# Convolution outputs and z gates of a hybrid decoder layer: ScalarE's Silu function in place of tanh and products

## The chip, the cores and the metric

The kernel runs on one core of a Trainium2 chip, in one launch. The metric is the device time of that launch in microseconds (us). TensorE is called PE below, VectorE DVE, ScalarE ACT, GpSimd POOL and SyncE SP, as in the profile.

## The reference, cut to what matters

One layer of a hybrid decoder for 512 prompt tokens and 8 sequences of 8 sample tokens, 576 columns in all, with a width of 1024. One projection of the normed input feeds two groups of heads: a Mamba-2 group (SSD: z, x, B, C, dt) and an RWKV-7 group. What the change touches is the activation behind the causal convolution and the gate z:

```
z, xbc, dt_raw, rw = jnp.split(proj, IN_SPLITS, axis=-1)
conv = depthwise_conv4(concat(conv_buf, xbc)) + conv_b
xbc_act = jax.nn.silu(conv)                       # x, B, C of the SSD group
...
yg = y.reshape(b, l, SSD_WIDTH) * jax.nn.silu(z)  # gate, then a grouped norm
```

Around it stand the chunked SSD scan, the RWKV-7 recurrence in chunks (a triangular solve among them), W_out, a SwiGLU block, a gated per-layer embedding and a last norm. All of it is in fp32; each fp32 operand of a large product is split into a high and a low part, and three matmuls are summed.

## The kernel before, in words

A tile has 128 channels on the partitions and the 576 tokens along the free axis. `projections()` (line 65) lists the 128-channel tiles of the input projection in the order in which PE makes them. The RWKV group is done in four quarters of heads, called q0 to q3 here; each has tiles of its own, and between them stand tiles of the SSD group: 12 convolution tiles `("xbc", c)`, one dt tile, and 8 z tiles. `FILL = (5, 5, 3, 0)` gives q0 four convolutions and dt, q1 five, q2 three. The z tiles come last: some within q3, some at the start of the SSD part.

A quarter runs `prep` (line 529: the lora tiles of decay, a and gate, with Tanh and Exp on ACT, and the scan of the log decay on DVE, line 561, whose result `lo` ACT turns into `pb` with Exp), `gram` (line 601), `bonus`, `decayed`, `inverse` (line 921, with the triangular solve on DVE in `solve`, lines 674 and 676), `chain` (line 739, the recurrence over chunks) and `head_norm`. In `prep` and `gram` the filler tiles give PE dense work between small operations of DVE, ACT and POOL; in q0 and q1 the last fillers lie beside DVE's solve. The chain of one quarter overlaps the preparation of the next. So there are three stretches, one for each of q0, q1 and q2, in which PE waits often.

The kernel is written with the Tile framework, whose scheduler simulates a timeline and sets the order of every engine's queue from it; only the order in which the code is written and the buffers of the pools steer it. A change in the code can therefore move instructions that it does not name. Each engine works through its own queue in order: an instruction that waits holds up all behind it.

A convolution tile (`conved`, line 376) takes the projection out of PSUM into `E` (two ACT copies, 128x512 and 128x64), POOL puts the old state in front and copies the new state `cso` out, ACT makes the first tap `h`, DVE adds three taps (line 395). The SiLU of v is written as (tanh(v/2) + 1) * v/2: the weights and the bias in `hw` are halved at the start (line 172), so `h` is v/2; ACT makes `th` = Tanh(h); DVE forms (th + 1) * h in two pieces, 512 prompt columns (line 400) and 64 sample columns (line 401), into E's place, and a DMA writes it out. E, h and th share a pool of three buffers (`cslot`, line 278), so a convolution holds all three until that DMA is done.

A z tile (`zed`, line 404) goes the same way without a convolution: an ACT copy with scale 0.5 (`hz`), an ACT Tanh with scale 0.5 (`thz`), a DVE product (line 411), and a DMA. ACT's functions need a table; `ACT_TABLE_LOAD` in the queue switches it. Tanh and Exp are used here without a load between them, Ln and the square roots have loads of their own. All calls of ACT go through the helper on line 93, so its instructions all carry L93.

Of the kernel before, what the change touches and what calls it, by code (L numbers as in the profile page):

```python
# [10 lines left out]
AF = mybir.ActivationFunctionType  # L11
ALU = mybir.AluOpType
# [4 lines left out]
P = 128  # L17
D = 1024
NT = 576
ND = 64  # L20
# [55 lines left out]
def hybrid_step(ctx, tc, A):  # L76
    nc = tc.nc
    V, S, G, T = nc.vector, nc.scalar, nc.gpsimd, nc.tensor
# [9 lines left out]
    def nm(s):  # L88
        uid[0] += 1
        return f"{s}_{uid[0]}"  # L90

    def act(out, in_, func=AF.Copy, scale=1.0, bias=0.0):
        return S.activation(out, in_, func, bias=bias, scale=scale)  # L93
# [9 lines left out]
    def lin_bank():  # L103
        turn[0] += 1
        return lins[turn[0] // 2 % len(lins)].tile([P, 1024], F32, tag="lin", name=nm("lin"))

    def lin_ps(off=224):
        return lin_bank()[:, off:off + NT]
# [8 lines left out]
    def const(name, shape, dt=F32):  # L117
        return cp.tile(shape, dt, tag=name, name=name)

    pv = const("pv", [P, PV_COLS])  # L120
# [47 lines left out]
    hw = const("hw", [P, 76])  # L168
    at, _ = PV["w0"]
    V.tensor_scalar(hw[:, 0:16], pv[:, at:at + 16], 0.5, None, ALU.mult)  # L170
    at, _ = PV["conv_w"]
    V.tensor_scalar(hw[:, 16:76], pv[:, at:at + 60], 0.5, None, ALU.mult)
    omu = const("omu", [P, 26])
    at, n = PV["shift_mu"]
    V.tensor_scalar(omu[:], pv[:, at:at + n], -1.0, 1.0, ALU.mult, ALU.add)
    hka = const("hka", [P, 16])
    at, n = PV["k_a"]
# [47 lines left out]
    def linear(xs, ps, order=None):  # L225

        nk = len(xs)
        for k in range(0, nk, 4):
            b = min(4, nk - k)
            hi, lo = wload(b)  # L230
            for n, (p, q) in enumerate(order or ()):
                for i in range(b):
                    for a, e in HV:
                        T.matmul(ps[:, a:e], (hi, lo)[p][:, i * P:(i + 1) * P], xs[k + i][q][:, a:e],  # L234
                                 start=n == k + i == 0, stop=n == 2 and k + i == nk - 1, skip_group_check=True)
            if order:
                continue
            for i in range(b):
                xh, xl = xs[k + i]
                mm3(ps, hi[:, i * P:(i + 1) * P], lo[:, i * P:(i + 1) * P], xh, xl, k + i == 0, k + i == nk - 1)  # L240
# [37 lines left out]
    def cslot(name, shape=None, dt=F32):  # L278
        return sp.tile(shape or [P, NT], dt, tag="cv", name=nm(name), bufs=3)
# [42 lines left out]
    def rstd_by_token(acc, scale, a=0, b=NT, banks=None):  # L322

        t = None if banks else lin_bank()
        ws = WIN if b - a == NT else [min(c, b - P) for c in range(a, b, P)]
        off = 64 if b - a == NT else -a
        st = banks[1][:, 200:200 + len(ws)] if banks else t[:, 700:700 + len(ws)]
        accs = acc if isinstance(acc, tuple) else (acc,)
        for n, q in enumerate(accs):
            for i, c in enumerate(ws):  # L330
                for h in (0, 64):
                    T.matmul(st[h:h + 64, i:i + 1], q[:, c + h:c + h + 64], ones[:, 0:1],
                             start=n == 0 and (i == 0 or len(accs) == 1), stop=n == len(accs) - 1,
                             skip_group_check=len(accs) > 1)
        rn = cp.tile([P, 5], F32, tag="rn5", name=nm("rn5"), bufs=2)
        roots.append(act(rn[:, 0:len(ws)], st, AF.Sqrt, scale=scale, bias=eps_t[:, 0:1]))
        V.reciprocal(rn[:, 0:len(ws)], rn[:, 0:len(ws)])
        for i, c in enumerate(ws):
            o = banks[c // 448][:, c % 448:c % 448 + P] if banks else t[:, c + off:c + off + P]
            T.transpose(o, rn[:, i:i + 1].to_broadcast([P, P]), ident[:])  # L340
        return None if banks else t[:, a + off:b + off]
# [34 lines left out]
    def conved(c):  # L376
        ps = lin_ps()
        linear(X, ps)
        cst = se.tile([P, 27], F32, tag="cst", name=nm("cst"), bufs=2)
        nc.sync.dma_start(cst[:], A["s_conv"][:, c, :])  # L380
        cso = se.tile([P, 27], F32, tag="cso", name=nm("cso"), bufs=2)
        E = cslot("E", [P, SLOT])
        e3 = E[:, 0:88].rearrange("p (b t) -> p b t", b=8)
        act(E[:, 91:SLOT], ps[:, ND:NT])
        act(e3[:, :, 3:11], ps[:, 0:ND].rearrange("p (b t) -> p b t", b=8))
        G.tensor_copy(e3[:, :, 0:3], cst[:, 0:24].rearrange("p (b t) -> p b t", b=8))
        G.tensor_copy(E[:, 88:91], cst[:, 24:27])
        G.tensor_copy(cso[:, 0:24].rearrange("p (b t) -> p b t", b=8), e3[:, :, 8:11])
        G.tensor_copy(cso[:, 24:27], E[:, 600:603])
        nc.sync.dma_start(A["o_conv"][:, c, :], cso[:])  # L390
        h = cslot("h", [P, 600])
        w = lambda i: hw[:, 16 + 4 * c + i:17 + 4 * c + i]
        act(h[:], E[:, 0:600], AF.Identity, scale=w(0), bias=hw[:, 64 + c:65 + c])
        for i in range(1, 4):
            V.scalar_tensor_tensor(h[:], E[:, i:i + 600], w(i), h[:], ALU.mult, ALU.add)  # L395
        th = cslot("th", [P, 600])
        act(th[:], h[:], AF.Tanh)
        o = E[:, 0:NT]
        h3, t3 = (t[:, 0:88].rearrange("p (b t) -> p b t", b=8)[:, :, 0:8] for t in (h, th))
        V.scalar_tensor_tensor(o[:, ND:NT], th[:, 88:600], 1.0, h[:, 88:600], ALU.add, ALU.mult)  # L400
        V.scalar_tensor_tensor(o[:, 0:ND].rearrange("p (b t) -> p b t", b=8), t3, 1.0, h3, ALU.add, ALU.mult)
        nc.sync.dma_start(xbc_d[c][:], o)

    def zed(c):
        ps = lin_ps()
        linear(X, ps)
        h = cslot("hz")
        act(h[:], ps, AF.Copy, scale=0.5)
        th = cslot("thz")
        act(th[:], ps, AF.Tanh, scale=0.5)  # L410
        V.scalar_tensor_tensor(h[:], th[:], 1.0, h[:], ALU.add, ALU.mult)
        nc.sync.dma_start(sz_d[c][:], h[:])

    def dts():
# [56 lines left out]
    def fill(n=1):  # L471

        for _ in range(min(n, len(todo))):
            which, c = todo.pop(0)
            if which == "xbc":
                conved(c)
            elif which == "z":
                zed(c)
            elif which == "dt":
                dts()  # L480
            else:
                Q[which].t.append(shifted(c, which == 0, which % 2 and len(Q[which].t) > 3))
# [773 lines left out]
    for what in SEQ:  # L1256
# [7 lines left out]
        elif what == "y":  # L1264
            for j in range(6):
                t = cslot("yl")
                nc.sync.dma_start(t[:], yr_d[j][:])
                YR.append(split(t[:], xp, ("xhi", "xlo"), [P, NT], lo_eng=G))
        else:
            ps = lin_ps()  # L1270
            linear(YR[0:6], ps)
            t = cslot("pr")
# [21 lines left out]
    for c in range(8):  # L1294
        ps = lin_ps()
# [48 lines left out]
    def ft(name):  # L1344
        return pools[-1].tile([P, NT], F32, tag="f", name=nm(name), bufs=9 if len(pools) > 1 else 6)
# [9 lines left out]
    for f in range(2):  # L1355
        ps = lin_ps()
# [20 lines left out]
    for k in range(4):  # L1377
        xa, xb, t = ft("xa"), ft("xb"), ft("tt")
        for x, c in ((xa, k), (xb, k + 4)):
            act(x[:], hs[c][:], AF.Identity, scale=par("norm_ffn", c))  # L1380
        t1, t2, t3, t4 = t[:, N1], t[:, N2], xa[:, N2], xb[:, N1]
# [97 lines left out]
    for a, b in ((0, 320), (320, NT)):  # L1479
# [18 lines left out]
        for c in range(8):  # L1498
# [5 lines left out]
            ps = lin_bank()[:, 0:n]  # L1504
# [8 lines left out]
            t = ft("pg")[:, 0:n]  # L1513
# [8 lines left out]
        ps = rstd_by_token(acc, 1.0 / D, 0, n)  # L1522
        rl = ft("rs")[:, 0:n]
        act(rl, ps)
        for c in range(8):
            h = hs[c][:, a:b]
# [146 lines left out]
```

## Time and profile before

| what | us |
|---|---|
| time, median of 3 runs | 1345.34 (1345.02 to 1348.39) |
| span of the profiled execution | 1349.0 |
| PE busy in it | 1246.8 (92 %) |
| DVE busy | 826.0 (61 %) |
| POOL busy | 625.6 (46 %) |
| ACT busy | 618.9 (46 %) |
| table loads, 25 in ACT's queue | 1.283 each |

Only the span is given for the profiled execution; it lies 0.27 % above the median of the timed runs and 0.05 % above the highest of them. In the profile a row of a group gives the line, the engine, the operation, output and inputs with their shapes, the count, then busy time and mean nanoseconds of one, then the idle time of the engine just before these instructions and who ended it. A row of the timeline starts with the instruction's start and its duration in us. A row of the waits names the instruction that waited and what it waited for, the total in us, the count, and the longest. "PEclk" is the granted TensorE clock as a share of full speed.

The three stretches with many waits lie at about 98 to 145 us (q0), 210 to 272 us (q1) and 350 to 412 us (q2). The z tiles lie between 530 and 630 us. From about 680 us to the end there is the SSD part, W_out, SwiGLU and the embedding, with PE at work almost throughout.

### The profile page before, as it was taken

What the parts mean: (1) busy time and instruction counts of PE and PEld (TensorE: products, weight loads), DVE (VectorE), ACT (ScalarE), POOL (GpSimd) and SP (SyncE); (2) the same over time, 40 slices, a digit from 0 to 9 for tenths busy, and PEclk for the clock granted to TensorE, in tenths of its full rate; (3) what the DMA queues carried; (4) which work ended last, traced back from release to release, by engine and by line L of the source; (5) the groups of instructions that cost most, each with busy time, mean ns of one, the idle gap of its engine ahead of it and who ended that gap; (6) DMA issues with size and microseconds to landing.
All of it is one profiled execution on the core that took longest, in us unless ns stands there. A gap on an engine that the chain in (4) does not pass through costs nothing.

```text
span 1349.0 us, 26596 instructions
## 1 busy us (share of the span) xinstructions
PE 1246.8 (92%) x10525; PEld 1150.7 (85%) x10525; DVE 826.0 (61%) x1443; ACT 618.9 (46%) x1256; POOL 625.6 (46%) x597
## 2 busy tenths in 40 slices
PE   6897999999989978899999969989999999999997
PEld 6787897889868957788779859889999999999997
DVE  6648666887687785943466667886553135443454
ACT  6565436534654463343434364464442124433363
POOL 5425413642355154122456645565654336654642
PEclk9897799899979978889989989998999999999998
DMA  5322242234232412262454542222323222314322
GB/s 164 125 68 66 77 117 63 85 103 116 75 99 78 109 41 80 94 214 83 157 176 131 179 125 72 73 93 88 92 88 87 79 86 82 93 59 149 96 89 71
DMA packets 94461, 135.58 MB, mean 100 GB/s; under 512 B 34705, under 2 KB 39057, under 8 KB 94337
## 3 DMA queue, kind: packets, MB, share of 16 engines
q1 hardware_dynamic: 93760, 133.36, 32.4%
q8 instruction: 83, 1.36, 0.4%
q10 hardware_dynamic: 576, 0.52, 0.1%
q14 instruction: 42, 0.34, 0.1%
HBM read 106.10 MB, written 27.75 MB: 99 GB/s over the span
## 4 chain that ended last, share of the span: by engine, by line
PE 63%; DVE 14%; ACT 4%; issue 4%; DMA 3%; POOL 3%; DVEq 0%; SPq 0%; ACTq 0%; POOLq 0%
PE lin L234 21%; PE lin L1403 8%; PE lin L223 6%; PE lin L221 6%; PE lin L222 6%; DVE h L395 2%; PE lin L1508 1%; PE lin L1509 1%; PE lin L1510 1%; DVE tmp L674 1%; DVE wlo L206 1%; DVE Tt L676 1%; PE lin L613 1%; PE cx L797 1%; DVE suv L831 1%
## 5 line engine op out<-in xcount | busy, mean ns | idle before, releaser
L206 POOL TENSOR_TENSOR wlo<-raw,whi 128x512 fp32r<-128x512 f32 (+1 forms) x108 | 146.4, 1356 | 352.5 <-ACT whi L93 269.5
L93 ACT ACTIVATE whi<-raw 128x512 fp32r<-128x512 f32 (+1 forms) x232 | 143.3, 618 | 259.1 <-PE lin L234 126.4
L221 PE MATMUL lin<-xhi,whi 128*128 128x288 f32 (+1 forms) x784 | 243.3, 311 | 2.5 <-ACT whi L93 2.2
L223 PE MATMUL lin<-xhi,wlo 128*128 128x288 f32 (+1 forms) x784 | 241.5, 308 | 2.3 <-POOL wlo L206 2.3
L222 PE MATMUL lin<-xlo,whi 128*128 128x288 f32 (+1 forms) x784 | 241.5, 308 | 0.3 <-POOL xlo L194 0.3
L206 DVE TENSOR_TENSOR wlo<-raw,whi 128x512 fp32r<-128x512 f32 (+1 forms) x124 | 100.9, 814 | 103.2 <-PE lin L234 60.4
L221 PEld LDWEIGHTS lin<-xhi,whi 128*128 128x128 f32 (+1 forms) x784 | 151.0, 193 | 9.3 <-ACT whi L93 2.6
L223 PEld LDWEIGHTS lin<-xhi,wlo 128*128 128x128 f32 (+1 forms) x784 | 150.7, 192 | 6.2 <-POOL wlo L206 2.8
L222 PEld LDWEIGHTS lin<-xlo,whi 128*128 128x128 f32 (+1 forms) x784 | 150.8, 192 | 4.8 <-issue 1.2
L234 PE MATMUL lin<-xhi,whi 128*128 128x288 f32 x384 | 62.3, 297 | 3.2 <-ACT xhi L93 3.0
L234 PE MATMUL lin<-xlo,whi 128*128 128x288 f32 x384 | 60.8, 298 | 0.0
L234 PE MATMUL lin<-xhi,wlo 128*128 128x288 f32 x384 | 59.3, 297 | 0.0
L234 PEld LDWEIGHTS lin<-xhi,whi 128*128 128x128 f32 x384 | 54.6, 189 | 3.8 <-ACT xhi L93 1.7
L234 PEld LDWEIGHTS lin<-xlo,whi 128*128 128x128 f32 x384 | 54.8, 191 | 0.0
L234 PE MATMUL lin<-ah,wlo 128*128 128x288 f32 x352 | 54.7, 296 | 0.0
L234 PE MATMUL lin<-al,whi 128*128 128x288 f32 x352 | 54.7, 296 | 0.0
L234 PE MATMUL lin<-ah,whi 128*128 128x288 f32 x352 | 54.7, 296 | 0.0
L234 PEld LDWEIGHTS lin<-xhi,wlo 128*128 128x128 f32 x384 | 54.3, 191 | 0.0
L1403 PE MATMUL lin<-T,wh 128*128 128x288 f32 x320 | 50.1, 296 | 4.5 <-DVE T L194 2.8
L674 DVE TENSOR_TENSOR tmp<-L,Tt 72x30 f32<-72x30 f32 (+14 forms) x120 | 49.2, 410 | 3.2
L234 PEld LDWEIGHTS lin<-ah,whi 128*128 128x128 f32 x352 | 49.6, 189 | 0.0
L234 PEld LDWEIGHTS lin<-ah,wlo 128*128 128x128 f32 x352 | 49.6, 189 | 0.0
(425 smaller groups left out, 3197.8 us busy)
## 6 DMA issues: line engine op xcount, KB each, us to landing
raw<-wts SPq DMA_DIRECT2D x271, 256.0 KB, 2.6
S<-s_wkv SPq DMA_DIRECT2D x8, 512.0 KB, 5.1
hd<-s_ssm SPq DMA_DIRECT2D x8, 512.0 KB, 4.5
o_ssm_s<-hd SPq DMA_DIRECT2D x8, 512.0 KB, 2.9
xbc_d<-E SPq DMA_DIRECT2D x12, 288.0 KB, 2.1
x<-xT SPq DMA_DIRECT2D x8, 288.0 KB
gate_d<-g SPq DMA_DIRECT2D x8, 288.0 KB, 2.5
bv_d<-rw SPq DMA_DIRECT2D x8, 288.0 KB
```

Of the source, the lines that this page charges most:

```text
L93: return S.activation(out, in_, func, bias=bias, scale=scale)
L206: eng.tensor_tensor(lo[:, 0:n], raw[:, 0:n], hi[:, 0:n].bitcast(F32), ALU.subtract)
L221: T.matmul(ps[:, a:b], whi, xhi[:, a:b], start=first, stop=False)
L222: T.matmul(ps[:, a:b], whi, xlo[:, a:b], start=False, stop=False)
L223: T.matmul(ps[:, a:b], wlo, xhi[:, a:b], start=False, stop=last)
L234: T.matmul(ps[:, a:e], (hi, lo)[p][:, i * P:(i + 1) * P], xs[k + i][q][:, a:e], start=n == k + i == 0, stop=n == 2 and k + i == nk - 1, sk ...
L395: V.scalar_tensor_tensor(h[:], E[:, i:i + 600], w(i), h[:], ALU.mult, ALU.add)
L613: T.matmul(ps[:, c:c + 128].rearrange("p (a t) -> p a t", a=2), s.BK[jj][H[e], g].rearrange("p a t -> p (a t)"), s.G[H[e], g, jj, :, e], s ...
L674: V.tensor_tensor(o, L[:, jx:jx + 1, jx + 1:32].to_broadcast([NB, jx, n]), Tt[:, 0:jx, jx:jx + 1].to_broadcast([NB, jx, n]), ALU.mult)
L676: V.tensor_tensor(Tt[:, 0:jx, jx + 1:32], Tt[:, 0:jx, jx + 1:32], o, ALU.subtract)
L797: T.matmul(uw[H[e], jj, :], TT[H[e], g, jj, :], xs[H[e], jj, :], start=True, stop=True)
L1403: T.matmul(ps, (hi, lo)[p][:, k * P:(k + 1) * P], OPS[n][k][q], start=first and p == q == k == 0, stop=p == 1 and k == 3, skip_group_check ...
```

## The change

The halving of the convolution's weights and bias becomes a plain copy, so `h` is v itself. ACT then writes Silu(h) straight into E's place, in the same two pieces; the tile `th` and both products on DVE are gone. The z gate becomes one ACT Silu from PSUM in place of copy, Tanh and product; `thz` is gone. A convolution now holds two of the pool's three buffers, a z tile one.

```diff
-    V.tensor_scalar(hw[:, 16:76], pv[:, at:at + 60], 0.5, None, ALU.mult)
+    V.tensor_copy(hw[:, 16:76], pv[:, at:at + 60])
...
-        th = cslot("th", [P, 600])
-        act(th[:], h[:], AF.Tanh)
         o = E[:, 0:NT]
-        h3, t3 = (t[:, 0:88].rearrange("p (b t) -> p b t", b=8)[:, :, 0:8] for t in (h, th))
-        V.scalar_tensor_tensor(o[:, ND:NT], th[:, 88:600], 1.0, h[:, 88:600], ALU.add, ALU.mult)
-        V.scalar_tensor_tensor(o[:, 0:ND].rearrange("p (b t) -> p b t", b=8), t3, 1.0, h3, ALU.add, ALU.mult)
+        h3 = h[:, 0:88].rearrange("p (b t) -> p b t", b=8)[:, :, 0:8]
+        act(o[:, ND:NT], h[:, 88:600], AF.Silu)
+        act(o[:, 0:ND].rearrange("p (b t) -> p b t", b=8), h3, AF.Silu)
         nc.sync.dma_start(xbc_d[c][:], o)
...
-        act(h[:], ps, AF.Copy, scale=0.5)
-        th = cslot("thz")
-        act(th[:], ps, AF.Tanh, scale=0.5)
-        V.scalar_tensor_tensor(h[:], th[:], 1.0, h[:], ALU.add, ALU.mult)
+        act(h[:], ps, AF.Silu)
```

Lines behind the convolution have a number lower by 5 afterwards (line 561 is then 556, and so on). DVE's queue goes from 1310 rows of such a listing to 1278; SP's keeps 517. ACT's table loads go from 25 to 40: Silu and Exp need a switch between them, Silu and a following Tanh do not. Of the 15 new loads four lie in q0, three in q1, three in q2, and five between the z tiles and the start of the SSD part.

ACT's queue in q0's `prep`, around the first convolution. `lo` is the log decay before and after the scan, `pb` its Exp, `whi` the high half of a weight for PE, `E` and `h` are the convolution's tiles, `G` are the rows that the gram products on PE read. Before:

```order
L93 ACTIVATE lo_1255<-lin_1248,hw 128x576
L93 ACTIVATE th_1092<-h_1087 128x600
L93 ACTIVATE pb_1258<-lo_1245 128x576
L93 ACTIVATE lo_1245<-lo_1245 128x576
L93 ACTIVATE whi_1326<-raw_1324 128x512
L93 ACTIVATE E_1220<-lin_1156 128x512
L93 ACTIVATE E_1220<-lin_1156 128x8x8
L93 ACTIVATE G_982<-ar_981 64x9x64 x2
```

The same place after the change:

```order
L93 ACTIVATE lo_1251<-lin_1244,hw 128x576
L93 ACT_TABLE_LOAD
L93 ACTIVATE E_1079<-h_1087 128x512
L93 ACTIVATE E_1079<-h_1087 128x64
L93 ACT_TABLE_LOAD
L93 ACTIVATE pb_1254<-lo_1241 128x576
L93 ACTIVATE lo_1241<-lo_1241 128x576
L93 ACTIVATE G_982<-ar_981 64x9x64 x2
L93 ACTIVATE whi_1322<-raw_1320 128x512
L93 ACTIVATE E_1218<-lin_1154 128x512
L93 ACTIVATE E_1218<-lin_1154 128x8x8
```

The Tanh became two Silu instructions with a load ahead of them and another ahead of `pb`; the pair of `G` now stands ahead of the next weight and of the next convolution's `E`.

DVE's queue in q1's `prep`. Line 561 is the scan that gives `lo`, line 206 the low half of a weight for PE, line 805 a small copy in the chain of q0, line 565 the product of `rw` with `pb`. Before:

```order
L561 SCALAR_TENSOR_TENSOR lo_2949<-rmask,lo_2949 128x576
L400 SCALAR_TENSOR_TENSOR E_2783<-th_2796,h_2791 128x512
L401 SCALAR_TENSOR_TENSOR E_2783<-th_2796,h_2791 128x64
L206 TENSOR_TENSOR wlo_3001<-raw_2998,whi_3000 128x512
L805 TENSOR_SCALAR suv_1704<-cx_1782 64x2x64
L565 TENSOR_TENSOR ar_2685<-rw_2542,pb_2962 128x576
```

The same place after the change:

```order
L556 SCALAR_TENSOR_TENSOR lo_2937<-rmask,lo_2937 128x576
L206 TENSOR_TENSOR wlo_2989<-raw_2986,whi_2988 128x512
L560 TENSOR_TENSOR ar_2677<-rw_2534,pb_2950 128x576
L513 COPY rx_2961<-rn_2791 128x512
L590 SCALAR_TENSOR_TENSOR lo_2812<-rw_2466,pv,lo_2812 128x576
L800 TENSOR_SCALAR suv_1698<-cx_1776 64x2x64
```

The pair of products is gone between the scan and the weight, and the chain's small copy now stands behind three large instructions in place of ahead of them.

ACT's queue around the first z tile of the SSD part. `smask` and `DEC` are Exp of decay sums, `xs`, `suv`, `ar` and `TT` belong to the last quarter's chain. Before:

```order
L93 ACTIVATE smask_7164<-smask_7164 16x576
L93 ACTIVATE xs_6656<-cx_6653 64x128
L93 ACTIVATE whi_7251<-raw_7249 128x512
L93 ACTIVATE TT_467<-cx_6580 32x16x32
L93 ACTIVATE whi_7281<-raw_7279 128x512
L93 ACTIVATE hz_7158<-lin_7097 128x576
L93 ACTIVATE thz_7160<-lin_7097 128x576
L93 ACTIVATE suv_6635<-cx_6659 64x2x64
L93 ACTIVATE DEC_7208<-cb_7183 128x192
```

The same place after the change:

```order
L93 ACT_TABLE_LOAD
L93 ACTIVATE smask_7125<-smask_7125 16x576
L93 ACTIVATE xs_6623<-cx_6620 64x128
L93 ACTIVATE whi_7212<-raw_7210 128x512
L93 ACTIVATE TT_467<-cx_6547 32x16x32
L93 ACTIVATE whi_7242<-raw_7240 128x512
L93 ACT_TABLE_LOAD
L93 ACTIVATE hz_7122<-lin_7061 128x576
L93 ACTIVATE suv_6602<-cx_6626 64x2x64
L93 ACTIVATE ar_5944<-cx_6631 128x2x64
L93 ACT_TABLE_LOAD
L93 ACTIVATE DEC_7169<-cb_7144 128x192
```

Copy and Tanh became one Silu, and three loads stand ahead of `smask`, of `hz` and of `DEC`.

## Prediction

> **What bounds the kernel now.** I read the page's busy shares first, to see which engine sets the time over the whole span:
>
> ```profile
> span 1349.0 us, 26596 instructions
> PE 1246.8 (92%) x10525; PEld 1150.7 (85%) x10525; DVE 826.0 (61%) x1443; ACT 618.9 (46%) x1256; POOL 625.6 (46%) x597
> ```
>
> PE is busy for 92 %: only about 102 us are left in which it stands still, and only those, and slow clock, can be won by a change that takes nothing from PE. So I asked where they lie, with the windows view cut at the stages. Its columns are start and end, length, then the busy us of PE, of its weight loads, DVE, ACT and POOL, and the granted clock, the DMA share and GB/s:
>
> ```profile
> 98.00:145.00 47.00, 36.25 (x257) 32.10 (x258) 33.90 (x46) 25.15 (x47) 30.90 (x39) 0.68 0.25 65
> 145.00:210.00 65.00, 63.66 (x613) 60.10 (x613) 45.32 (x104) 25.29 (x53) 13.01 (x15) 0.97 0.34 97
> 210.00:272.00 62.00, 56.73 (x507) 46.18 (x503) 47.06 (x83) 40.53 (x88) 37.14 (x49) 0.89 0.27 78
> 350.00:412.00 62.00, 55.80 (x494) 45.62 (x493) 49.90 (x83) 39.77 (x86) 33.87 (x45) 0.83 0.24 75
> 530.00:606.00 76.00, 68.71 (x647) 60.26 (x647) 52.13 (x128) 27.45 (x60) 16.42 (x20) 0.87 0.49 151
> 680.00:1349.00 669.00, 636.77 (x5032) 615.76 (x5030) 364.66 (x506) 282.75 (x537) 360.57 (x273) 0.97 0.32 99
> ```
>
> The convolutions and z tiles all lie ahead of 680 us. In the first, third and fourth row, the preparation of q0, q1 and q2, PE idles for 10.8, 5.3 and 6.2 us at a granted clock of 0.68, 0.89 and 0.83; DVE is busy for 72, 76 and 80 %, ACT for 54, 65 and 64 %. No engine is full there: operations of four engines follow one another, and a single chain sets the time. Between them (second row, the solve of q0) PE is 98 % busy. Then I read what ends PE's waits in these stretches:
>
> ```profile
> PE lin L613 <- POOL bk L585: 2.6, 2, 1.9
> PE cx L698 <- DMA AA<-Ad: 1.3, 1, 1.3
> PE lin L613 <- ACT E L93: 1.4, 1, 1.4
> PE tr L769 <- ACT bkt L93: 3.0, 1, 3.0
> PE cx L789 <- DVE suv L831: 2.9, 1, 2.9
> ```
>
> The first is of q0's preparation, the second of its solve, the third of q2's, the last two of the z tiles' stretch. POOL, ACT and DVE each end some, so work taken from one of them pays only in places, and work given to another costs only in places.
>
> **The change part by part.** The groups with their prices:
>
> ```profile
> L93 ACT ACT_TABLE_LOAD x24 | 30.8, 1283 | 1.6 <-DVE rw L371 1.2
> L93 ACT ACTIVATE th<-h 128x600 f32<-128x600 f32 x12 | 8.4, 700 | 13.5 <-DVE h L395 13.4
> L93 ACT ACTIVATE E<-lin 128x512 f32<-128x512 f32 x12 | 7.1, 589 | 4.1 <-DVE E L401 4.0
> L93 ACT ACTIVATE E<-lin 128x64 f32<-128x64 f32 x12 | 2.6, 220 | 0.0
> L93 ACT ACTIVATE thz<-lin 128x576 f32<-128x576 f32 x8 | 5.1, 643 | 0.0
> L93 ACT ACTIVATE hz<-lin 128x576 f32<-128x576 f32 x8 | 5.1, 639 | 0.3 <-PE lin L223 0.2
> L400 DVE SCALAR_TENSOR_TENSOR E<-th,h 128x512 f32<-128x512 f32 x12 | 11.3, 939 | 0.0
> L401 DVE SCALAR_TENSOR_TENSOR E<-th,h 128x64 f32<-128x64 f32 x12 | 5.2, 435 | 0.0
> L411 DVE SCALAR_TENSOR_TENSOR hz<-thz,hz 128x576 f32<-128x576 f32 x8 | 6.1, 766 | 5.1 <-ACT thz L93 5.1
> ```
>
> DVE loses 11.3 + 5.2 + 6.1 = 22.6 us. ACT: no Silu is in this trace. Tanh (643 ns for 576 columns) costs what a copy does (639), so I take Silu at the price of the copies of its own shapes: 589 + 220 ns for 700, at most 0.11 us more for a convolution, and 0.64 us less for a z tile, about -4 us together. Were Silu dearer by half, the 24 pieces and 8 z would add about 7 us of ACT, whose share of the path would be the ends below. The 15 loads are the real price. What follows a load is seen where a z tile has one:
>
> ```profile
> 583.23 0.65 ACT L93 ACTIVATE hz<-lin 128x576 f32<-128x576 f32 x1
> 583.90 1.28 ACT L93 ACT_TABLE_LOAD   x1
> 585.19 0.65 ACT L93 ACTIVATE thz<-lin 128x576 f32<-128x576 f32 x1
> ```
>
> The Tanh starts 1.29 us after its load's start, so 15 loads take 15 x 1.3 = 19.5 us of ACT, which gets some 15.5 us more work in all. The Trainium skill ("ScalarE: Activation LUTs", What ACT_TABLE_LOAD costs) puts a drain of about 1380 ns beside the 1283 ns of the load, 2.66 us for each switch. By that rule ACT would lose an estimated 15 x 2.66 = 39.9 us; the rows above show the load at the page's length and no such gap behind it, so I keep 1.3 us.
>
> DVE thus gives 22.6 us and ACT takes 15.5. What of it lies on the path is worked out by stage.
>
> *q0's preparation (98 to 145).* The pairs on DVE, and ACT beside the first of them:
>
> ```profile
> 107.49 0.72 ACT L93 ACTIVATE lo<-lin,hw 128x576 f32<-128x576 f32 x1
> 108.99 0.69 ACT L93 ACTIVATE pb<-lo 128x576 f32<-128x576 f32 x1 [0.19 <-DVE lo L561]
> 110.66 1.92 DVE L400 SCALAR_TENSOR_TENSOR E<-th,h 128x512 f32<-128x512 f32 x1
> 112.64 0.75 DVE L565 TENSOR_TENSOR ar<-rw,pb 128x576 f32<-128x576 f32 x1
> 121.32 0.68 DVE L400 SCALAR_TENSOR_TENSOR E<-th,h 128x512 f32<-128x512 f32 x1
> 122.06 0.74 DVE L579 SCALAR_TENSOR_TENSOR kk<-lo,kk 128x576 f32<-128x576 f32 x1
> ```
>
> The first pair held the queue for 112.64 - 110.66 = 1.98 us, the second for 122.06 - 121.32 = 0.74; a third like the second makes 3.46. Against that, ACT after `lo` (over at 108.21) has a load (to 109.5), two Silu (to 110.3), a load (to 111.6), and only then `pb`, 2.65 us later than 108.99. `pb` ends near 112.3, so the product `ar` that reads it gains 0.3 instead of 1.98; the weight and E behind `pb` on ACT come up to 2.3 us later, and PE waits for those. Another load stands ahead of the second convolution's Silu, in the same queue as the first tap of the third. Bounds: -0.5 (only the later pairs count) to +2.7 (the whole delay of `pb` goes through). I take 0: POOL's `bk`, for which PE waits, has DVE gains ahead of it and ACT losses.
>
> *Solve of q0 (145 to 210).* The fourth convolution's pair stood amid DVE's solve, 0.74 us by the short form above. PE waits for the solve's result for 1.3 us only, so no more can be had. An Exp load ahead of dt's is new, 1.3 us if it lies on the path. Value -0.7, bounds -1.3 and +1.3.
>
> *q1's preparation (210 to 272).*
>
> ```profile
> 229.48 0.77 ACT L93 ACTIVATE lo<-lo,eps_t 128x576 f32<-128x576 f32 x1
> 233.63 0.68 ACT L93 ACTIVATE pb<-lo 128x576 f32<-128x576 f32 x1 [0.69 <-DVE lo L561]
> 233.52 1.68 DVE L400 SCALAR_TENSOR_TENSOR E<-th,h 128x512 f32<-128x512 f32 x1
> 236.49 0.68 DVE L206 TENSOR_TENSOR wlo<-raw,whi 128x512 fp32r<-128x512 f32 x1
> 237.53 1.54 DVE L565 TENSOR_TENSOR ar<-rw,pb 128x576 f32<-128x576 f32 x1
> ```
>
> Here the pair held DVE for 236.49 - 233.52 = 2.97 us at the end of the scan, with `ar` behind it, and `pb` was done at 234.31, long before `ar` at 237.53. The load and Silu ahead of `lo` on ACT (1.3 us) come ahead of the scan; the load ahead of `pb` falls partly into the 0.69 us for which ACT waited: `pb` comes some 0.5 to 1.8 us later and is still ahead of the old `ar`. So `ar` starts 1.4 to 2.7 us earlier. The small chain copy (L805) now stands behind `ar`, but with the pair gone no later than before. A later pair adds 0.74, another the same: at most 2.97 + 2 x 0.74 = 4.4 us. A third load, ahead of the next convolution's Silu, hits rows of q0's chain on ACT. Bounds: -4.4, and +4.2 if all three loads (3.9) and the piece of Silu beyond the Tanh (3 x 0.1) go through. I take -1.5, near the low end of `ar`'s gain, for the DVE queue behind it is only one of the chains there.
>
> *q2's preparation (350 to 412).*
>
> ```profile
> 366.78 1.53 DVE L400 SCALAR_TENSOR_TENSOR E<-th,h 128x512 f32<-128x512 f32 x1
> 368.37 0.75 DVE L579 SCALAR_TENSOR_TENSOR kk<-lo,kk 128x576 f32<-128x576 f32 x1
> ```
>
> 1.59 us for the first pair and 0.74 for each of two more, 3.1 at the least and 4.4 by the price of q1's. ACT's new order puts a load and Silu ahead of the rows `G` from `pb` and of the next E, and PE already waits 1.4 us for an E of ACT here. Value 0, bounds -4.4 and +4.2.
>
> *z tiles (530 to 606, and on).* Three products (0.77 each) lie beside the last solve on DVE and leave it: 2.3 us, of which PE's 2.9 us wait for `suv` may lose some. The z tile shown above has load and one Silu in place of copy, load and Tanh: -0.65 us ahead of `bkt`, for which PE waits 3.0. The other loads, ahead of `smask`, z4, DEC and z5, each delay rows of the last chain by up to 1.3 us; z tiles lose a Copy or a Tanh of 0.64 each. Value -1.2, bounds -2.3 - 0.65, about -3, and +4 (three of the loads).
>
> *Elsewhere*: the copy of `hw` costs what the halving did. After 680 us nothing is changed. The fuller pool (a convolution keeps two of three buffers) lets the next E start before the DMA out is done; no wait of PE here is put down to that, so 0.
>
> Sum: 0 - 0.7 - 1.5 + 0 - 1.2 = -3.4 us on the profiled execution's span, 1349.0 to 1345.6. That span lies 0.27 % above the median of the runs; from that median, 1345.34 - 3.4 = 1341.9, and I give that. About 0.3 %, 4 us, is what a measurement of this kernel can tell from no change.
>
> **The rivals.**
> A, the forecast: gain on DVE and loads on ACT nearly cancel, 1341.9; its own range is 1337 to 1347. Chance 0.43.
> B: DVE's queue bounds the three preparations, and ACT's loads fit into its idle time. For it: DVE is the busiest engine beside PE in them, and ACT has a third of the time free. Against: `pb` in q0. Then q1 and q2 give 4.4 each, q0 0.5, with solve and z as above: -(8.8 + 0.5 + 0.7 + 1.2) = -11.2, 1334. Chance 0.30.
> C, slower: ACT's in-order queue becomes the bound of the preparations. Each Silu is fenced by a load on either side, and `pb`, `G`, the weight and E behind them come late; PE stalls. It decides where `pb` starts over 2 us after its scan in q0, q1 and q2. Then q0 +2.7, q1 +4.2, q2 +4.2, less the 1.9 of solve and z: +9.2, 1354.5. For it: the new order of ACT in q0; PE's waits on ACT in q2. Against: in q1 ACT idled just ahead of `pb`. Chance 0.25.
> D: the change doesn't do what it says, Silu being built of other instructions. The new queue has one instruction for each Silu, so 0.02 is left; 1345.
>
> **How the numbers follow.** Of A about 0.10 lies over 4 us below the median, 0.32 within, 0.01 above. B: 0.29 faster, 0.01 same. C: 0.22 slower, 0.03 same. D: same. So faster 0.39, same 0.38, slower 0.23. The range goes from just below B, 1333, to C, 1355; it leaves out the outer halves of B's and C's spread, a little under 2 in 10. A's own range stands above.
>
> **What would show it.** Right: 40 loads of 1.28 us with the next activation 1.3 us behind; Silu at 0.59 and 0.22 us; `pb` in q0 near 2.6 us after its scan, `ar` 0.3 us earlier; q1's stretch shorter by 1 to 3 us, q0's and q2's by under 1 either way; PE's `suv` and `bkt` waits in the z stretch shorter. Wrong: q0 or q2 longer by over 2.5 us with PE waiting on ACT's E, `G` or weights (C), or q1 and q2 both shorter by over 3 (B). A change of over 3 us behind 680 us would mean that the scheduler's new order, not the operations, set the result; I have no term for that.

## The result, and the profile after

| kernel | median us | runs | lowest to highest |
|---|---|---|---|
| before | 1347.26 | 7 | 1336.73 to 1348.39 |
| after | 1355.93 | 7 | 1353.65 to 1362.96 |

The changed kernel is slower: the ratio to before is 1.0083, with a 95 % interval of 1.0059 to 1.0108, some 11 us by the ratio. 1341.9 was forecast, and the range ended at 1355.0.

The profiled execution of the changed kernel, from the top of its page:

```profile
span 1357.6 us, 26563 instructions
PE 1249.7 (92%) x10525; PEld 1153.0 (85%) x10525; DVE 809.7 (60%) x1411; ACT 634.0 (47%) x1275; POOL 619.8 (46%) x597
```

ACT has 15.1 us more than before, and 15.5 were worked out. DVE has only 16.3 less where 22.6 were worked out: its 32 products are gone, but other instructions of DVE take longer (the 124 low halves of weights of line 206, 841 ns each in place of 814, make up 3.4 us). The groups of ACT show where its time went. Columns: busy us, mean ns of one, idle time ahead of them and who ended it.

```profile
L93 ACT ACT_TABLE_LOAD x39 | 50.0, 1283 | 3.0 <-DVE rw L371 1.2 <-DVE h L395 0.8 <-DVE smask L1021 0.3
L93 ACT ACTIVATE E<-h 128x512 f32<-128x512 f32 x12 | 7.6, 630 | 13.3 <-DVE h L395 13.2
L93 ACT ACTIVATE hz<-lin 128x576 f32<-128x576 f32 x8 | 5.1, 641 | 0.0
L93 ACT ACTIVATE E<-h 128x64 f32<-128x64 f32 x12 | 2.9, 242 | 0.0
```

With the one of line 125 there are 40 loads. Silu takes 630 and 242 ns where 589 and 220 were taken, and 641 for z. (The prediction says that no Silu stands in the trace of before. That was an oversight: SwiGLU there has Silu instructions, 687 ns for 128x576; the price does not change by it.)

Two profiles of one kernel can differ by more than the change is worth. A second profile of the kernel before, taken later, has a span of 1339.6 us at a mean granted clock of 0.947, the first one 1349.0 at 0.940; the span lies 1.7 us below the execution's own time in both profiles that list the two. So I cut the traces into stages that mean the same in each and set both profiles of before beside the one of after. A stage ends where PE starts the combine of a quarter's inverse (line 698, then 693), the last but one where the last quarter's head norm starts (line 901, then 896). The lengths are differences of these starts:

| stage ends at | before | before, second profile | after |
|---|---|---|---|
| combine of q0 (prep and solve of q0) | 192.8 | 190.3 | 191.8 |
| combine of q1 (prep of q1 and its solve) | 149.1 | 149.2 | 148.2 |
| combine of q2 | 137.9 | 138.4 | 140.1 |
| combine of q3 (z0 to z3 lie here) | 108.6 | 107.8 | 115.0 |
| head norm of q3 (z4 to z7) | 86.5 | 86.4 | 89.2 |
| end | 674.1 | 667.5 | 673.3 |

The three preparations, about which most of the prediction argues, are within 2.5 us. The largest loss lies in the fourth row: 6.4 or 7.2 us against two executions of before that differ there by 0.8. The fifth row adds 2.7 or 2.8. The last row says nothing: after is 0.8 us shorter there than one profile of before and 5.8 longer than the other. The end of the fourth row, first in the second profile of before, then in the one of after: DVE's last instruction of the solve, and PE's first combine.

```profile
570.38 0.20 DVE L676 TENSOR_TENSOR Tt<-Tt,tmp 72x30 f32<-72x30 f32 x1
...
585.68 1.92 PE L698 MATMUL cx<-AA,Lst 32*32 32x32 f32 x64
```

```profile
572.23 0.21 DVE L671 TENSOR_TENSOR Tt<-Tt,tmp 72x30 f32<-72x30 f32 x1
...
595.13 1.92 PE L693 MATMUL cx<-AA,Lst 32*32 32x32 f32 x64
```

From the start of the solve's last instruction to the combine it is 15.3 us before and 22.9 after. The solve is not late: PE has not yet finished q2's chain. In before, a step of that chain is queued ahead of the start-state products of q3 (`cb<-G,S`, line 734). The rows of PE there, first profile of before:

```profile
515.50 0.61 PE L789 MATMUL cx<-suv,G 128*128 128x128 f32 x4
518.45 2.76 PE L734 MATMUL cb<-G,S 64*64 64x16 f32 x48 [2.34 <-DMA S<-s_wkv]
```

After, those products (now line 729) come first and the step (now line 784) behind them:

```profile
517.46 0.87 PE L729 MATMUL cb<-G,S 64*64 64x16 f32 x22 [1.14 <-DMA S<-s_wkv]
...
522.81 0.48 PE L729 MATMUL cb<-G,S 64*64 64x16 f32 x4
523.22 1.64 PE L608 MATMUL lin<-G,bk 64*128 64x128 f32 x10
524.79 0.79 PE L784 MATMUL cx<-suv,G 128*128 128x128 f32 x2
```

It is a pure matter of order: neither instruction is touched by the change. From there on the chain is one step behind. z0 starts near 533 us in both, and before it three steps of q2's chain are left, after it four. A step among z tiles takes 11 to 16 us (between the starts of this product in the two profiles), so when the z tiles are used up PE stands alone with the rest of the chain. The waits of PE between the last two combines, second profile of before, then after (total us, times, longest):

```profile
PE cx L797 <- DVE xs L792: 2.1, 1, 2.1
PE cx L797 <- ACT xs L93: 0.8, 2, 0.5
```

```profile
PE cx L792 <- DVE xs L787: 3.9, 2, 2.2
PE cx L792 <- ACT xs L93: 3.4, 3, 2.2
```

The same product, `xs` with the inverse, waited 2.9 us and now waits 7.3. PE's waits for `bkt` and `suv` in this stretch did become shorter, as the prediction listed among its signs (3.0 to 2.3 us, 2.9 to 0.6), but that is less than what `xs` adds.

### The profile page after: what moved, and what is told of

Read it like the earlier page. It is cut to its first block, busy times and chain, and to the rows that moved or that the text cites. A ratio compares the mean times of both kernels' runs of the same rounds, so it can differ in the third digit from the quotient of the medians.

```text
span 1357.6 us, 26563 instructions
## 1 busy us (share of the span) xinstructions
PE 1249.7 (92%) x10525; PEld 1153.0 (85%) x10525; DVE 809.7 (60%) x1411; ACT 634.0 (47%) x1275; POOL 619.8 (46%) x597
## 4 chain that ended last, share of the span: by engine, by line
PE 67%; DVE 15%; ACT 7%; DMA 5%; issue 4%; POOL 2%; SPq 0%; DVEq 0%; ACTq 0%; POOLq 0%
PE lin L234 22%; PE lin L1398 8%; PE lin L221 7%; PE lin L223 7%; PE lin L222 7%; DVE Tt L671 1%; PE lin L608 1%; DVE tmp L669 1%; DVE wlo L206 1%; ACT L93 1%; DMA raw<-wts 1%; ACT G L93 1%; PE cx L792 1%; PE cx L807 1%; PE cx L784 1%
## 5 line engine op out<-in xcount | busy, mean ns | idle before, releaser
L206 DVE TENSOR_TENSOR wlo<-raw,whi 128x512 fp32r<-128x512 f32 (+1 forms) x124 | 104.3, 841 | 103.7 <-PE lin L234 60.6
L234 PEld LDWEIGHTS lin<-al,whi 128*128 128x128 f32 x352 | 49.6, 189 | 0.0
```

What stands on the lines that cost most here:

```text
L206: eng.tensor_tensor(lo[:, 0:n], raw[:, 0:n], hi[:, 0:n].bitcast(F32), ALU.subtract)
```

## The experiments

Theory L: the 15 loads stand on the path. Theory O: the scheduler, given other durations, put the queues in another order, and that order costs the time. The first test uses that Tanh in place of Silu leaves every queue as it is but for the loads; the traces confirm it, for DVE, ACT and POOL run the same instructions in the same order in after and tanh_direct, and in before, silu_products and conv_loads. So two functions with and without the products make a table of four.

**tanh_direct**, the queues of after without the 15 loads:

```diff
-        act(o[:, ND:NT], h[:, 88:600], AF.Silu)
+        act(o[:, ND:NT], h[:, 88:600], AF.Tanh)
...
-        act(h[:], ps, AF.Silu)
+        act(h[:], ps, AF.Tanh)
```

> The changed kernel with Tanh in place of Silu in the convolutions and z tiles (the output is tanh of v in place of v times sigmoid of v). Every engine has the instructions of the changed kernel in its order, only ACT lacks the 15 new table loads. Theory L, the loads stand on the path: without them the loss goes and DVE's 22.6 us less shows, 1338 to 1345 us, ratio to before 0.995 to 0.999. Theory O, the scheduler's new order and the missing products set the loss by themselves (PE's pieces of the third quarter's chain against the z tiles at 500 to 560 us): 1351 to 1357 us, ratio 1.004 to 1.008, and the delay against before still jumps by 4 to 6 us between 500 and 560.

Measured: 1353.62 us, ratio 1.0074 (1.0053 to 1.0096). Theory O. With less work on DVE and no more on ACT, the kernel is still slower than before. The stage with z0 to z3 takes 111.1 us, 2.5 or 3.3 more than before: the jump of 4 to 6 us did not come in that size. The solve ends earlier here, and the distance from its last instruction to the combine is as long as in after, 22.9 us. The rest of the loss is not located by this profile.

**silu_products**, the queues of before with the 15 loads:

```diff
-        act(th[:], h[:], AF.Tanh)
+        act(th[:], h[:], AF.Silu)
...
-        act(th[:], ps, AF.Tanh, scale=0.5)
+        act(th[:], ps, AF.Silu, scale=0.5)
```

> The kernel before with Silu in place of both Tanh, products kept (the output is (silu(h)+1)*h). Every engine has the instructions of before in its order, ACT has 15 more table loads and nothing else is moved. Theory L: slower by 8 to 15 us, 1354 to 1362, ratio 1.006 to 1.011. Theory O: the loads hide for the most part, slower by 0 to 3 us, ratio 1.000 to 1.002.

Measured: 1351.01, ratio 1.0038 (1.0015 to 1.0060). Between the two expectations: loads cost something too, some 5 us of their 19.5. Much of it is seen in the stage with z4 to z7, where four of the 15 new loads lie: it takes 90.2 us, against 86.4 to 86.7 in the two profiles of before and in conv_loads (below), which have the same queues without those four. 1.1 to 1.4 us of that are gaps of PE, the rest is longer busy time of the same matmuls.

**conv_only** and **z_only**, the two edits apart:

```diff
-        act(h[:], ps, AF.Silu)
+        act(h[:], ps, AF.Copy, scale=0.5)
+        th = cslot("thz")
+        act(th[:], ps, AF.Tanh, scale=0.5)
+        V.scalar_tensor_tensor(h[:], th[:], 1.0, h[:], ALU.add, ALU.mult)
```

> Only the 12 convolutions by Silu, the z gates as before. The two traces lie within 1.7 us of each other up to 530 us and part at the z tiles and the last quarter. If the z edit costs the loss (loads of z0 to z2 and at the SSD part, or the order there): 1342 to 1348, ratio 0.997 to 1.001. If what the convolutions do to the order behind them costs it: 1351 to 1357, ratio 1.004 to 1.008.

> Only the 8 z gates by Silu, the convolutions as before. If the z edit costs the loss: 1351 to 1357, ratio 1.004 to 1.008, with the jump of 4 to 6 us at 500 to 560 us. If the convolutions cost it: 1342 to 1348, ratio 0.997 to 1.001.

Measured: conv_only 1360.99, ratio 1.0109 (1.0074 to 1.0145); z_only 1350.82, ratio 1.0040 (1.0018 to 1.0062). Each edit alone makes the kernel slower. The loss in the stage with z0 to z3 comes with the edit of the convolutions, which lie 100 us and more ahead of it: conv_only has no new load at a z tile, and that stage takes 117.2 us in it, the longest so far. With z alone it takes 107.8, as before. This is what an order that shifts with early durations looks like, and not what a load would do. The loss of z_only, at the edge of what was expected if the z edit were to blame, lies elsewhere: its stage with z4 to z7 takes 90.2 us, as in silu_products.

**held**, the changed kernel with the one step put back (behind that place the scheduler orders the queues anew):

```diff
-        start_states(s)
+        with tc.issue_after(marks[2, 4].ins) if s.q == 3 else nullcontext():
+            start_states(s)
```

> The changed kernel with one ordering constraint: PE's start-state products of the last quarter (line 729) are queued behind step 4 of the third quarter's chain, where they stood before the change. All queues are as in the changed kernel up to that place; behind it the chain stands ahead of the first z tile by one step more. Order theory: the step lost at the z tiles (combine of the last quarter 23 us behind the end of its solve in place of 15) comes back, 4 to 8 us, 1347 to 1352, ratio to before 1.001 to 1.005, and that distance is 18 us or less. Rival: PE has the same work in all, and the wait returns further on: 1353 to 1358, ratio 1.006 to 1.009.

**held_tanh**, the same without loads:

> The same constraint with Tanh in place of Silu in the convolutions and z tiles (the output is tanh of v in place of v times sigmoid of v): the queues of the run held without the 15 new loads. Order theory with loads as a second cause: 3 to 6 us below held, 1343 to 1348, ratio to before 0.998 to 1.003. Rival, loads cost nothing: as held within 2 us. Rival, the order in the first quarters is to blame and not this place: 1351 to 1355, as the run without the constraint.

Measured: held 1351.39, ratio 1.0063 (1.0033 to 1.0092); held_tanh 1346.61, ratio 1.0009 (0.9981 to 1.0037). The stage goes to 109.1 and 109.0 us. The combine of held:

```profile
567.11 0.20 DVE L671 TENSOR_TENSOR Tt<-Tt,tmp 72x30 f32<-72x30 f32 x1
...
584.90 1.80 PE L693 MATMUL cx<-AA,Lst 32*32 32x32 f32 x64 [0.30 <-DVE ar L907]
```

17.8 us in place of 22.9: the distance came back as expected. The time is less plain. For held, the microseconds lie in the range of the order theory and the ratio in that of the rival, and the intervals of after and held overlap, so that pair shows no gain. The pair without loads has one clear of noise (1.0074 to 1.0009), but between their profiles the stage shortens by only 2.1 us (111.1 to 109.0), and other instructions moved with the step. So how much of the gain is due to the step itself is not shown. Between held and held_tanh loads cost 0.54 %. And the place is not all: held_tanh lacks DVE's 32 products, has no new load, and is no faster than before. Other shifts in the order remained.

**before_again** and **conv_loads**, the baseline and 10 of the 15 loads:

```diff
-        act(th[:], h[:], AF.Tanh)
+        act(th[:], h[:], AF.Silu)
```

> The kernel before, unchanged, for a second profile of it: the first had a span of 1349.0, at the upper end of its runs. 1338 to 1350; where a second execution has the last combine at 15 to 16 us behind the end of the solve again, that distance belongs to the order and not to the execution.

> The kernel before with Silu in place of Tanh in the convolutions alone, products kept (the convolution's output is (silu(h)+1)*h): 10 of the 15 loads, all queues as before otherwise. If loads in the preparations carry the cost that the run with all 15 showed (ratio 1.0038): ratio 1.003 to 1.005. If the five at the z tiles carry it: 0.999 to 1.001.

Measured: before_again 1341.98, ratio 0.9998 (0.9966 to 1.0030), and its profile has the 15.3 us shown above, so that distance belongs to the order. conv_loads 1345.40, ratio 1.0012 (0.9987 to 1.0036): with products kept, the convolutions' ten loads cost nothing that these runs can tell. The ratio lies between the two expectations, and its interval holds both.

The last four separate the order from the edit. Once the whole program is written, a table gives each engine's instructions in the order of before, and each is tied behind the one ahead of it (issue order only, no wait):

```diff
+        for p in range(1, len(row)):
+            tc.add_manual_dep(have[f"I-{row[p]}"], f"I-{row[p - 1]}", mybir.DependencyInfo(
+                mybir.DependencyClass.NoSync, mybir.DependencyReason.DATA), reason="listed")
...
             hybrid_step(ctx, tc, A)
+            queue_as_listed(nc, tc)
```

**listed** is the changed kernel in the order of before, **listed_tanh** the same with Tanh, **listed_conv** the edit of the convolutions alone in that order, **before_reordered** the kernel before with PE and DVE in the order of after.

> The changed kernel with every engine's queue put in the order that it has before the change (the place of a Silu is that of its Tanh, the products are simply gone, the 15 loads stay where a switch asks for them). If the new order was the larger cause: 1340 to 1347, ratio to before 0.998 to 1.003, some 8 us under the changed kernel. If the loads are: 1348 to 1354, ratio 1.004 to 1.008.

> The same with Tanh in place of Silu (the output is tanh of v in place of v times sigmoid of v): the queues of before without the 32 products on DVE and without new loads, so that nothing but the 22.6 us of DVE is gone. If DVE's share bounds the preparations, 4 to 11 us under before, 1332 to 1339, ratio 0.992 to 0.997. If it does not, 1340 to 1345, ratio 0.998 to 1.001. The difference to the run listed is the price of the loads in the order of before.

> The kernel before, products and Tanh kept, with the queues of PE and DVE in the order of the changed kernel (the products where they come ready; ACT, POOL and SP as the scheduler then puts them). If the order by itself costs what the runs with and without the held chain say: 1350 to 1356, ratio 1.005 to 1.010. If the order costs only where ACT also has loads: 1342 to 1347, ratio 0.999 to 1.003.

> The convolutions by Silu, the z gates by Tanh and products, every queue in the order of before: 10 of the 15 loads, 24 of the 32 products gone. The convolutions' loads alone cost 0.12 percent with products kept. If leaving out those products is worth anything in this order, 1334 to 1341, ratio 0.993 to 0.998, and it beats both kernels; else 1342 to 1347, ratio 0.999 to 1.003.

| kernel | queues as in | loads | products on DVE | median us | ratio to before, 95 % |
|---|---|---|---|---|---|
| listed_tanh | before | 25 | none | 1336.97 | 0.9947 (0.9927 to 0.9966) |
| before_again | before | 25 | 32 | 1341.98 | 0.9998 (0.9966 to 1.0030) |
| listed | before | 40 | none | 1345.62 | 1.0012 (0.9995 to 1.0029) |
| silu_products | before | 40 | 32 | 1351.01 | 1.0038 (1.0015 to 1.0060) |
| listed_conv | before | 35 | 8 | 1347.53 | 1.0026 (1.0007 to 1.0044) |
| tanh_direct | after | 25 | none | 1353.62 | 1.0074 (1.0053 to 1.0096) |
| after | after | 40 | none | 1355.93 | 1.0083 (1.0059 to 1.0108) |
| before_reordered | after, PE and DVE | 25 | 32 | 1374.46 | 1.0228 (1.0188 to 1.0267) |

In the order of before, the change as a whole costs 0.12 %, which is no difference. It is made of two parts: products gone, -0.53 % or 7 us, and loads, 1.0012 - 0.9947 = 0.65 % or 9 us. The step from listed to after, 1.0083 - 1.0012 = 0.71 % or some 9.5 us, is the order; without loads it is 1.0074 - 0.9947 = 1.27 %. By their intervals, each of these differences is good to about 0.3 %. before_reordered only says that an order can cost 30 us for a program that it wasn't made for; it is no price of this one, and it missed its expectation on the far side. A version that beats before was not found: listed_conv was meant to be one and is 0.26 % slower.

The stage with z0 to z3 in four kernels, from combine to combine: second profile of before, after, listed, listed_tanh. Columns: start and end, length, busy us of PE, weight loads, DVE, ACT, POOL, granted clock, DMA share, GB/s.

```profile
477.90:585.70 107.80, 91.39 (x885) 74.61 (x884) 76.35 (x174) 45.86 (x107) 37.04 (x41) 0.81 0.27 82
```

```profile
480.20:595.10 114.90, 94.84 (x884) 77.63 (x884) 76.69 (x173) 46.73 (x106) 37.83 (x43) 0.80 0.27 76
```

```profile
479.60:583.50 103.90, 89.12 (x882) 72.27 (x882) 74.29 (x172) 45.63 (x105) 36.91 (x41) 0.84 0.30 86
```

```profile
474.50:576.90 102.40, 86.54 (x884) 70.04 (x884) 74.21 (x172) 44.07 (x104) 37.16 (x41) 0.87 0.31 89
```

PE's work is the same in all four. PE idles for 20.1 us in after, 16.4 in before, 14.8 in listed. listed and after are 11.0 us apart in this stage, nearly their whole difference in span (1346.1 and 1357.6); tanh_direct and listed_tanh, the same pair without loads, are 8.7 apart in it (111.1 and 102.4). The other rows of these four profiles show that the new order does not only lose: with loads and without, q1's is 3.4 and 3.0 us shorter than in the order of before, q2's 3.8 and 4.3 longer, that of z4 to z7 1.0 and 2.1 longer. Of the 11.0 us, 5.3 are gaps, 5.7 are the same matmuls taking longer (89.1 and 94.8 us) at a granted clock of 0.84 and 0.80. What sets that clock isn't shown: the gaps don't do it alone, for in listed_tanh they are 15.9 us at 0.87.

## Why the prediction was wrong, point by point

**The sum came near in the order that it was made for, but not within the noise.** It was -3.4 us with the queues as in before; listed measures +0.12 % (-0.05 to +0.29), that is -1 to +4 us, some 5 us more than the sum. "Gain on DVE and loads on ACT nearly cancel" is what the runs show, 7 us against 9. But the text had priced the two only together, stage by stage, so a sum near zero does not confirm its single terms.

**The step that failed is the one on the z tiles**, "Value -1.2, bounds ... about -3, and +4", and with it "After 680 us nothing is changed", which treats the order as given. The two rows with the z tiles are longer by 9.1 or 10.0 us, 6.4 or 7.2 of them in the first, outside the bounds, and not by what they were made of. The bounds came from loads and products taken in the order of before. What the runs showed in their place is the order: by the time of listed and after it costs 0.71 %, some 9.5 us, and in the first of the two rows the edited kernel takes 103.9 us in the order of before (listed) and 115.0 in its own. There a step of q2's chain stands behind q3's start states, and the combine comes 22.9 us behind the solve in place of 15.3. The text named this at its end, "the scheduler's new order, not the operations", and said that it had no term for it; but it looked for it behind 680 us, where the two profiles of before differ by 6.6 us and nothing can be read. It should have had a term: the quoted rows of DVE in q1 already showed a chain copy that had moved behind three large instructions, and the same comparison of PE's queue at the z tiles would have shown the chain one step further back.

**q0's preparation, right.** Rows of after, to set beside those of 107 to 113 us in before:

```profile
108.48 1.28 ACT L93 ACT_TABLE_LOAD   x1
109.78 0.78 ACT L93 ACTIVATE E<-h 128x512 f32<-128x512 f32 x2
110.57 1.28 ACT L93 ACT_TABLE_LOAD   x1
111.87 0.69 ACT L93 ACTIVATE pb<-lo 128x576 f32<-128x576 f32 x1
```

```profile
107.35 1.87 DVE L556 TENSOR_TENSOR_SCAN lo<-rmask,lo 128x576 f32<-128x576 bf16 x1 [1.86 <-ACT lo L93]
...
112.59 0.76 DVE L560 TENSOR_TENSOR ar<-rw,pb 128x576 f32<-128x576 f32 x1 [1.59 <-ACT pb L93]
```

The scan in before:

```profile
107.09 1.87 DVE L561 TENSOR_TENSOR_SCAN lo<-rmask,lo 128x576 f32<-128x576 bf16 x1 [1.83 <-ACT lo L93]
```

After the change the scan ends at 107.35 + 1.87 = 109.22 and `pb` starts 2.65 us behind it, as forecast; `ar` starts 5.24 us behind the start of the scan, against 5.55 in before (107.09 to 112.64), so the expected gain of 0.3 us came. Of the 1.98 us of the pair, 1.59 went into a wait for ACT. The load is 1.28 us with the next activation 1.30 behind its start: the trace went on disagreeing with the drain of which the Trainium skill ("ScalarE: Activation LUTs", What ACT_TABLE_LOAD costs) speaks.

**q1 and q2, inside their bounds, and no more can be said.** q1's stage is 1 us shorter (-1.5 was forecast), q2's some 2 longer (0, and under 1 either way as a sign). But z_only has the queues of before up to 540 us, and its q1 stage takes 152.5 us against 149.1 and 149.2, so one profile doesn't settle 1 or 2 us. Scan and `ar` in q1:

```profile
232.82 1.44 DVE L556 TENSOR_TENSOR_SCAN lo<-rmask,lo 128x576 f32<-128x576 bf16 x1 [0.35 <-ACT lo L93]
235.97 1.95 DVE L560 TENSOR_TENSOR ar<-rw,pb 128x576 f32<-128x576 f32 x1
```

In before:

```profile
231.84 1.76 DVE L561 TENSOR_TENSOR_SCAN lo<-rmask,lo 128x576 f32<-128x576 bf16 x1
```

Behind the start of the scan `ar` comes 3.15 us in place of 5.69, a gain of 2.5, inside the forecast 1.4 to 2.7. But the scan itself, with the load and Silu ahead of its `lo`, comes 41.0 us behind q0's combine in place of 39.0, so of the gain only 0.5 us is left.

**The rivals.** C gave 1354.5 and the kernel took 1355.93, but not by C: it put the loss into q0, q1 and q2, at 2.7 to 4.2 each, and those are within 2.5 of before. B's claim that loads fit into ACT's idle time is wrong in the order of before, where with the products gone they cost 9 us. Its other half holds in part: DVE's products were worth 7 us, but not 4.4 in each of q1 and q2: there listed_tanh has 149.7 and 136.0 us, before 149.1 and 137.9. In the stage with z0 to z3 it has 102.4, against 105.0 to 108.6 in the four profiles with products, the queues of before and no other edit than loads.

**What stays open.** Why loads cost 0.65 % in the order of before with products gone, 0.38 % with them, and 0.09 % in the order of after, was not taken apart; with intervals of 0.2 to 0.3 % on either side they overlap, so it is not even shown that the three differ. The lists fix the issue order of every engine, and with it what buffers the scheduler hands out; the two were not separated. What in the order of after costs its 9.5 us beside the chain step, and how much the step costs by itself, was not settled.

## What to carry to other kernels

Where a scheduler makes the queues, the sum over touched instructions is the answer to another question: what the change would cost in the old order. Compare the new order with the old also far behind the edit, at the stages whose chain ends late, and above all what moved against a dense filler; a chain that fell one step back there put the combine 22.9 us behind the solve in place of 15.3. To test the edit by itself, tie the queues into the old order: here that showed a change worth nothing inside a loss of 0.8 %.

## What the runs showed of the hardware that was not expected

Two profiles of the same kernel before differ by 9.4 us of span (1349.0 and 1339.6), at a granted clock of 0.940 and 0.947; 2.8 us of it lie ahead of the last head norm, 6.6 behind. A single pair of traces is therefore read by stages, and a difference no larger than that between two profiles of one kernel doesn't count. Two profiles can also agree by luck: q1's stage takes 149.1 and 149.2 us in them, and 152.5 in z_only, which has the same queues up to 540 us.
